# A two-layer S5/SSD trunk in fp32: x reloaded one tile a step, panel buffers shared between two phases, two more early pairs, a later spread

## The chip, the cores and the metric

The kernel runs on one core of one Trainium2 chip. The metric is the time of one execution on the device in microseconds (us). Names of engines: PE is TensorE, DVE is VectorE, ACT is ScalarE, POOL is GpSimd, SP is SyncE; in this kernel SP does nothing but issue DMAs.

## The reference

A trunk of two layers over one sequence of 1024 tokens and 1024 channels, all in float32. Each layer is a mixer (S5 in the first, Mamba-2 SSD in the second) followed by an MLP, each with an RMSNorm and a modulation (shift, scale, gate) in front, and a last RMSNorm closes it. What the change touches is the MLP:

```python
def _sq_relu_mlp(h, w1, w2):
    a = jax.nn.relu(h @ w1)      # w1: 1024 x 4096
    return (a * a) @ w2          # w2: 4096 x 1024
...
h = _modulate(_rmsnorm(x, norm_mlp_g[i]), sh2, sc2)
x = x + g2 * _sq_relu_mlp(h, mlp_w1[i], mlp_w2[i])
```

## The kernel before

**Arithmetic.** Every fp32 product is made of three matmuls of fp32r parts: `split` has ACT cast a tile to its high part (L84) and DVE subtract to get the low part (L85), and `mm3` multiplies high by high, high by low and low by high (L117 to L119). Both MLP products are done in 2x2 blocks with seven block products in place of eight, so there are panels that are sums and differences of blocks.

**The two MLP phases.** The up phase (`Up`) goes through 16 pairs m of column blocks of w1. `rows` loads and combines the weights of a pair, `pair` does its products and writes seven panels of the result (`put`, `minus`) to HBM scratch `bscr`, on POOL's DMA queue. A pair m below `UPS` has two of its seven products done earlier: while `up_second` (a generator) still builds the panels t1, t2, t3, t4 and b22 of h, each of its yields runs one `early(m)`, 24 matmuls whose results go to `sscr` and `cscr`; `pair` loads them again (L552, L553, the tiles `s` and `b12`) and does 60 matmuls. A pair m from `UPS` on does all of its 84. With `UPS` 12, the pairs 12 to 15 are of the second sort.

The down phase (`mlp_down`) has seven products q of eight steps s. One step is 24 matmuls that read one weight unit of w2 and one panel: `raw_w` and `raw_b` load them on SP's queue, three steps ahead; `prepare` splits them, two steps ahead (`h01h` and `h11h` are the high parts of a panel of step 0, `h21h` and `h31h` of step 1, `h41h` and `h51h` of step 2, `h61h` and `h71h` of step 3; step 4 reuses the tiles of step 0, and so on). After a product `evacuate` adds its four banks to x. x is not kept over the up phase: `up_save` writes it to `hscr` (named `xscr` in `mlp_down`), and in steps 2 to 5 of the first product `x_load` (L267) brings it back, 16 tiles of 256 KB, four a step, on SP's queue.

**Buffers.** Pool `K.wz` lives over both phases of an MLP, pool `K.br` only over the down phase (it is made after the pools `K.to` and `K.tp` of the up phase are released). A panel is a tile `br` of `K.br`, four buffers. The tiles `a22h` and `a22l` of the up phase lie in `K.wz`, two buffers each.

**Order.** The code is written as one stream, and a scheduler orders each engine's instructions from it, so that an SP row can stand ahead of one that the code has earlier. An engine, and SP's queue too, then works strictly in its order: a row that waits holds all rows behind it. SP's DMAs share eight completion semaphores in turn, so that a DMA also waits until the one eight before it has landed.

**The norm behind the first MLP.** `mid` is `norm_steps` (L200), a generator that is advanced two yields a step in product 5: squares of x summed to `ss`, column sums on PE, `rsqrt` on DVE in some ten small operations (`rsy`, L137 to L143), two yields, then `spread` (L156), four small matmuls (eight in the trace) that PE can do only when `rsy` is there, then the scaled tiles. `up_second` has two yields of the same kind ahead of its first use of `pb`.

Of the kernel before, what the change touches and what calls it, by code (L numbers as in the profile page):

```python
# [11 lines left out]
F32 = mybir.dt.float32  # L12
F32R = mybir.dt.float32r
# [6 lines left out]
P = 128  # L20
D = 1024
L = 1024
HT = 512
KT = D // P
EARLY = 5
DOWN = "b11", "t3", "t2", "b22", "t1", "t4", "b21"
UPS = 12
EPS = 1e-5
MAGIC = 12582912.0
TWO_PI = 6.283185  # L30
# [22 lines left out]
def half_of(half):  # L53
    return slice(half * HT, half * HT + HT)


def blk(i, n=P):
    return slice(i * n, i * n + n)
# [19 lines left out]
def tmp(K, name):  # L78
    return K.tmp.tile([P, 512], F32, tag="t", bufs=6, name=name)
# [51 lines left out]
def rsqrt(K, y, v):  # L131

    V = K.nc.vector
    n = v.shape[1]
    i = K.tmp.tile([P, n], I32, tag="rsi", name="rsi")
    t = K.tmp.tile([P, n], F32, tag="rst", name="rst")
    V.tensor_scalar(i, v.bitcast(I32), 1, None, op0=ALU.logical_shift_right)  # L137
    V.tensor_scalar(i, i, -1, 0x5F3759DF, op0=ALU.mult, op1=ALU.add)
    yy = i.bitcast(F32)
    for _ in range(3):  # L140
        V.scalar_tensor_tensor(t, yy, -0.5, yy, op0=ALU.mult, op1=ALU.mult)
        V.tensor_tensor(t, t, v, op=ALU.mult)
        V.scalar_tensor_tensor(y, t, 1.5, yy, op0=ALU.add, op1=ALU.mult)  # L143
        yy = y
# [55 lines left out]
def norm_steps(K, x, half, each, bank, order):  # L200

    nc = K.nc
    ss = K.br.tile([P, HT], F32, tag="ss", name="ss", bufs=1)
    for n, k in enumerate(order):
        if n == 0:
            nc.scalar.activation(ss, x[k][half], AF.Square)
        else:
            sq = tmp(K, "sq")
            nc.scalar.activation(sq, x[k][half], AF.Square)
            nc.vector.tensor_tensor(ss, ss, sq, op=ALU.add)  # L210
        yield
    yield
    pt = bank(K)
    for j in range(4):
        nc.tensor.matmul(pt[:, j:j + 1], ss[:, blk(j)], K.ones, start=True, stop=True)
    v = K.tmp.tile([P, 4], F32, tag="rsv", name="rsv")
    nc.vector.tensor_scalar(v, pt[:, 0:4], 1.0 / D, EPS, op0=ALU.mult, op1=ALU.add)
    y = K.tmp.tile([P, 4], F32, tag="rsy", name="rsy")
    rsqrt(K, y, v)
    yield  # L220
    yield
    pb = spread(K, y, bank)
    for k in range(KT):
        each(k, pb)
        yield
# [15 lines left out]
def h_tile(K, k, half, s, dtype=F32R):  # L241

    nm = f"h{k}{half}{'hl'[s]}"
    return K.hp.tile([P, HT], dtype, tag=nm, name=nm)
# [19 lines left out]
def x_load(K, x, src, ks=range(KT)):  # L264
    for k in ks:
        for f in range(2):
            K.nc.sync.dma_start(x[k][f], src[k, :, half_of(f)])  # L267
# [141 lines left out]
def up_second(K, pan, pool, x, G, sh, save):  # L409


    nc, V = K.nc, K.nc.vector

    def panel(nm):
        return [
            tuple(pool.tile([P, HT], F32R, tag=f"{nm}{j}{s}", name=f"{nm}{j}{s}") for s in "hl") for j in range(4)
        ]

    pan.b22 = [(h_tile(K, 4 + j, 1, 0), h_tile(K, 4 + j, 1, 1)) for j in range(4)]
    pan.t1 = [(h_tile(K, j, 1, 0), h_tile(K, j, 1, 1)) for j in range(4)]  # L420
    pan.t4, pan.t3, pan.t2 = panel("t4"), panel("t3"), panel("t2")
    up_save(K, x, 1, save)
    dsh = K.tmp.tile([P, 4], F32, tag="dsh", name="dsh")
    V.tensor_tensor(dsh, sh[:, 4:8], sh[:, 0:4], op=ALU.subtract)
    pb = rstd_half(K, [x[k][1] for k in range(KT)])
    yield
    yield
    for j in range(4):
        t11, t12, t21, t22 = x[j][0], x[j][1], x[4 + j][0], x[4 + j][1]
        for k in (j, 4 + j):  # L430
            V.scalar_tensor_tensor(x[k][1], x[k][1], G[:, k:k + 1], pb, op0=ALU.mult, op1=ALU.mult)
        V.tensor_tensor(t11, t12, t11, op=ALU.subtract)
        t2 = tmp(K, "t2")
        V.scalar_tensor_tensor(t2, t22, sh[:, 4 + j:5 + j], t11, op0=ALU.add, op1=ALU.subtract)
        split(K, *pan.t2[j], t2)
        V.scalar_tensor_tensor(t21, t21, sh[:, 4 + j:5 + j], t2, op0=ALU.add, op1=ALU.subtract)
        yield
    for j in range(4):
        t12, t22 = x[j][1], x[4 + j][1]
        V.scalar_tensor_tensor(t12, t22, dsh[:, j:j + 1], t12, op0=ALU.add, op1=ALU.subtract)  # L440
        split(K, *pan.t3[j], t12)
        if j % 2:
            yield
    for j in range(4):
        split(K, *pan.t1[j], x[j][0])
    yield
    for j in range(4):
        split(K, *pan.t4[j], x[4 + j][0])
    yield
    for j in range(4):  # L450
        shift_split(K, x[4 + j][1], pan.b22[j], sh[:, 4 + j:5 + j])
    yield
    yield
# [8 lines left out]
class Up:  # L462
# [9 lines left out]
    def bank(self, m):  # L472
        K = self.K
        return (K.ps if m % 4 < 2 else K.psb).tile([P, 512], F32, tag="ps", name="px")
# [39 lines left out]
    def early(self, m, pan):  # L514

        nc = self.K.nc
        u0 = unit(self.K, self.w1[of_pair(m)[0]])
        X, Z = self.bank(m), self.second_bank()
        self.product(X, u0, 0, pan.b11, True)
        s1 = self.held(X, "s1")  # L520
        nc.gpsimd.dma_start(self.sscr[m], s1)
# [3 lines left out]
    def rows(self, m, pool, late):  # L525

        K, V, g = self.K, self.K.nc.vector, SimpleNamespace()
        r0, r1 = [unit_raw(K, self.w1[i]) for i in of_pair(m)]
        g.u0 = unit_of(K, r0) if late else None
        g.a22 = tuple(pool.tile([P, HT], F32R, tag="a22" + s, name="a22" + s, bufs=2) for s in "hl")  # L530
        split(K, *g.a22, r1[:, HT:])
        V.tensor_tensor(r1[:, HT:], r1[:, 0:HT], r1[:, HT:], op=ALU.add)
        V.tensor_tensor(r1[:, 0:HT], r0[:, 0:HT], r1[:, 0:HT], op=ALU.subtract)
        V.tensor_tensor(r0[:, 0:HT], r1[:, HT:], r0[:, 0:HT], op=ALU.subtract)
        V.tensor_tensor(r0[:, HT:], r0[:, HT:], r0[:, 0:HT], op=ALU.subtract)
        g.u1 = unit_of(K, r0)
        g.u2 = unit_of(K, r1)
        return g

    def pair(self, m, g, pan, ahead):  # L540

        K = self.K
        X = self.bank(m)
        if g.u0:
            s = None
            self.product(X, g.u0, 0, pan.b11, True)
            b12 = self.held(X, "s1")
            Z = self.second_bank()
# [33 lines left out]
def mlp_down(K, pool, x, bscr, w2, gate, xscr, mid, extra):  # L582
# [7 lines left out]
    nc, V = K.nc, K.nc.vector  # L590
# [18 lines left out]
        return raws  # L609

    def raw_b(q, s):
        t = pool.tile([P, 2, HT], F32, tag="br", name="br", bufs=4)
        nc.sync.dma_start(t, bscr[q][s].rearrange("a p t -> p a t"))
        return t

# [66 lines left out]
    prepare(1)  # L682
    norms = iter(())
    X = None
    for n, (q, s) in enumerate(steps):
        load(n + 3)
        if q == 0 and 1 < s < 6:
            for k in (s - 2, s + 2):
                x_load(K, x, xscr, [k])
        prepare(n + 2)  # L690
        (wh, wl), b = ready.pop(n)
        if s == 0:
            X = X if q == 4 or q == 2 else banks(q)
            if q == 0:
                first = X
            if q in (2, 4):
                X = first
        for j in range(2):
            for i in range(4):
                c = blk(2 * i + j)  # L700
                mm3(
                    K, X[i], [(wh[:, c], wl[:, c], *b[j])],
                    q not in (2, 4) and s == 0 and j == 0, s == 7 and j == 1, more=True,
                )
        if s == 7:
            for i in range(4):
                evacuate(q, i, X[i])
        if q == 4 and s == 7:
            norms = mid(0, lambda K: K.ps.tile([P, 512], F32, tag="ps", name="pn"), range(KT))
        elif q == 5 or q == 6 and s < 3:  # L710
            next(norms, None)
            next(norms, None)
        elif q == 6:
            if s == 3:
                drain(norms)
                norms = mid(1, pss, [1, 3, 5, 7, 0, 2, 4, 6])
            if s < 7:
                next(norms)
        extra()
# [680 lines left out]
def trunk(ctx: ExitStack, tc: tile.TileContext, io, out):  # L1400
# [26 lines left out]
    K.bscr = [[[scr(f"b{i}{q}{s}", [2, P, HT]) for s in range(8)] for q in range(7)] for i in range(2)]  # L1427
    K.cscr = scr("cscr", [UPS, P, HT])
    K.sscr = scr("sscr", [UPS, P, HT])
    K.hscr = [scr(f"hscr{i}", [8, P, L]) for i in range(2)]  # L1430
# [10 lines left out]
    def mlp(i, x, xa, up, pan, gate, mid, cond=None, mods=(), gates=()):  # L1441
# [8 lines left out]
        for m in range(16):  # L1450
            ahead = []
            up.pair(m, rows, pan, lambda: m < 15 and ahead.append(up.rows(m + 1, K.wz, m + 1 >= UPS)))
            rows = ahead and ahead[0]
# [118 lines left out]
    def entry(i, x, G, sh):  # L1572
# [3 lines left out]
        def mid(f):  # L1576
            if f == 0:
                up.pan = up_first(K, x, G, sh, K.hscr[i])
            else:
# [4 lines left out]
                for _ in up_second(K, up.pan, K.tp, x, G, sh, K.hscr[i]):  # L1584
                    up.early(m, up.pan)
                    m += 1
                assert m == UPS

# [187 lines left out]
```

## Time and profile before

| what | value |
|---|---|
| time, median of 3 runs | 2564.22 us (2563.97 to 2564.57) |
| time of the profiled execution | 2565.46 us |
| its span in the trace | 2563.6 us |
| PE busy | 2453.4 us, 96% of the span, 11624 matmuls |
| DVE busy | 1914.1 us, 75% |
| ACT busy | 1151.5 us, 45% |
| POOL busy | 192.2 us, 7% |
| DMA queue of SP | 390.54 MB, 47.4% of the 16 DMA engines' time |
| DMA queue of POOL | 96.49 MB, 11.2% |

The span is what the trace covers; the profiled execution's own time is 1.9 us longer. PE is busy nearly all of the time, so the time can change where PE stands idle, and where its granted clock is below full. The idle time of the other engines counts only where PE waits for them.

### The profile page before, as it was taken

Reading aid. Unit: us, or ns where it says so; the run is one execution under the profiler, and the core shown is the slowest. Engines: PE = TensorE matmul, PEld = TensorE weight load, DVE = VectorE, ACT = ScalarE, POOL = GpSimd, SP = SyncE. Lnnn points to the kernel's source line nnn. Section 1 sums busy time; section 2 is a strip of 40 time slices with the busy share of each in tenths; the row PEclk is TensorE's granted clock in tenths of the full one; section 3 lists DMA queues with packets and bytes.
Section 4 is the critical chain, followed back from the end, with each engine's and each line's share of the span. In section 5 each row is a group of like instructions: output and inputs, shape, how many; then the busy total and the mean of one; then the engine's idle time right before and its main releaser. Section 6 shows DMA issues by size and latency. Waiting matters only on the chain.

```text
span 2563.6 us, 32608 instructions
## 1 busy us (share of the span) xinstructions
PE 2453.4 (96%) x11624; PEld 1964.4 (77%) x11624; DVE 1914.1 (75%) x3269; ACT 1151.5 (45%) x1903; POOL 192.2 (7%) x360
## 2 busy tenths in 40 slices
PE   7999999999997999999999999999999999799997
PEld 2787788777785888777888888878887778588886
DVE  8797754968777997958596868788687777576664
ACT  4586412743433443534464655544264443244442
POOL 0010000122220000100000000000011222100000
PEclk8999999999998999999999999999999999899998
DMA  6576772457759979723555554574236665873762
GB/s 240 157 165 175 243 234 86 156 206 259 255 183 338 314 260 317 251 75 114 160 158 158 160 175 141 181 245 131 86 128 210 224 217 183 303 218 126 259 204 68
DMA packets 284322, 497.49 MB, mean 194 GB/s; under 512 B 21760, under 2 KB 162048, under 8 KB 284160
## 3 DMA queue, kind: packets, MB, share of 16 engines
q1 hardware_dynamic: 245376, 390.54, 47.4%
q0 software_dynamic: 29184, 96.49, 11.2%
q10 hardware_dynamic: 9600, 8.39, 1.0%
q8 instruction: 91, 1.49, 0.2%
q14 instruction: 71, 0.58, 0.1%
HBM read 360.07 MB, written 131.07 MB: 192 GB/s over the span
## 4 chain that ended last, share of the span: by engine, by line
issue 41%; PE 36%; DVE 9%; DMA 9%; POOL 2%; ACT 2%; SPq 0%; POOLq 0%; DVEq 0%; ACTq 0%
PE pd L118 3%; PE pd L117 3%; PE pd L119 3%; PE py L117 3%; DMA ada<-in_ada 3%; PE py L118 3%; PE py L119 3%; DMA raw<-in_w 2%; PE px L117 2%; PE px L119 2%; PE px L118 2%; DVE wlo L85 2%; PE pm L117 1%; PE pm L119 1%; PE pv L119 1%
## 5 line engine op out<-in xcount | busy, mean ns | idle before, releaser
L84 ACT CAST whi<-raw 128x1024 fp32r<-128x1024 f32 x241 | 250.8, 1047 | 345.8 <-PE pd L118 145.0
L85 DVE TENSOR_TENSOR wlo<-raw,whi 128x1024 fp32r<-128x1024 f32 x241 | 292.8, 1216 | 113.7 <-ACT whi L84 112.9
L333 DVE SCALAR_TENSOR_TENSOR ada<-ada,cond 128x1024 f32<-128x1024 f32 x88 | 107.1, 1220 | 52.1 <-DMA ada<-in_ada 51.9
L498 ACT ACTIVATE s<-s 128x512 f32<-128x512 f32 x72 | 45.5, 632 | 171.4 <-DVE s L496 171.3
L1229 DVE SCALAR_TENSOR_TENSOR cacc<-cr,conv,cacc 128x1024 f32<-128x1024 f32 x72 | 91.6, 1278 | 0.9 <-ACT cacc L1210 0.8
L390 POOL DMA_DIRECT2D hscr<-x x32 | 17.4, 542 | 958.2 <-DVE x L730 754.9
L1282 ACT ACTIVATE L<-csb,cs 128x128 f32<-128x128 f32 x224 | 69.9, 390 | 39.8 <-DMA csb<-csr 39.7
L505 POOL DMA_DIRECT2D b<-s x96 | 52.0, 542 | 346.0 <-ACT s L499 244.2
L496 DVE TENSOR_TENSOR s<-s,px 128x512 f32<-128x512 f32 x56 | 38.3, 683 | 52.3 <-PE px L119 29.9
L496 DVE TENSOR_TENSOR s<-s,pv 128x512 f32<-128x512 f32 x40 | 27.4, 686 | 49.6 <-PE pv L119 49.4
L117 PE MATMUL py<-h01h,whi 128*128 128x512 f32 x64 | 27.3, 427 | 31.5 <-ACT h01h L84 31.5
L505 POOL DMA_DIRECT2D b<-tt x96 | 52.0, 542 | 46.1 <-DVE tt L510 33.4
L499 ACT ACTIVATE s<-s 128x512 f32<-128x512 f32 x72 | 45.6, 633 | 2.3
L1233 ACT ACTIVATE cth<-cacc 128x512 f32<-128x512 f32 x48 | 27.7, 624 | 40.3 <-DVE cacc L1229 40.3
L84 ACT CAST h01h<-br 128x512 fp32r<-128x512 f32 x28 | 17.4, 620 | 57.2 <-DMA br<-b 28.8
L1209 ACT COPY cr<-pd 128x512 f32<-128x512 f32 x48 | 27.8, 580 | 31.8 <-PE pd L119 31.6
L665 DVE SCALAR_TENSOR_TENSOR x<-py,mod,x 128x512 f32<-128x512 f32 x40 | 27.2, 744 | 20.0 <-PE py L119 20.0
L117 PE MATMUL pd<-h00h,whi 128*128 128x512 f32 (+1 forms) x97 | 39.9, 414 | 2.1 <-ACT h00h L237 1.8
L1302 DVE SCALAR_TENSOR_TENSOR y<-xs,cst,pm 128x128 f32<-128x128 f32 x128 | 38.2, 340 | 4.8 <-PE pm L1299 4.8
L1100 ACT ACTIVATE gt<-pd,bgh 128x512 f32<-128x512 f32 x16 | 11.0, 685 | 65.0 <-PE pd L119 65.0
L117 PEld LDWEIGHTS py<-h01h,whi 128*128 128x128 f32 x64 | 13.1, 204 | 35.2 <-ACT h01h L84 32.4
L117 PE MATMUL pd<-h01h,whi 128*128 128x512 f32 x97 | 39.4, 406 | 0.5 <-DVE h61h L730 0.5
(991 smaller groups left out, 8185.6 us busy)
## 6 DMA issues: line engine op xcount, KB each, us to landing
raw<-in_w SPq DMA_DIRECT2D x200, 512.0 KB, 4.6
br<-b SPq DMA_DIRECT2D x112, 512.0 KB, 4.9
ada<-in_ada SPq DMA_DIRECT2D x96, 512.0 KB, 5.0
b<-s POOLq DMA_DIRECT2D x96, 256.0 KB, 2.3
b<-tt POOLq DMA_DIRECT2D x96, 256.0 KB, 3.2
csb<-csr SPq DMA_DIRECT2D x32, 512.0 KB, 4.5
raw<-in_w_xbc SPq DMA_DIRECT2D x24, 512.0 KB, 4.7
xscr<-cacc SPq DMA_DIRECT2D x24, 512.0 KB, 2.7
```

Of the source, the lines that this page charges most:

```text
L84: K.nc.scalar.copy(hi, src)
L85: K.nc.vector.tensor_tensor(lo, src, hi.bitcast(F32), op=ALU.subtract)
L117: K.nc.tensor.matmul(ps, wh, xh, start=start and i == 0, stop=False, skip_group_check=more)
L118: K.nc.tensor.matmul(ps, wh, xl, start=False, stop=False, skip_group_check=more)
L119: K.nc.tensor.matmul(ps, wl, xh, start=False, stop=stop and i == n - 1, skip_group_check=more)
L333: K.nc.vector.scalar_tensor_tensor(r, r, 1.0, K.cond, op0=ALU.mult, op1=ALU.mult, accum_out=acc)
L496: nc.vector.tensor_tensor(t, t, p, op=ALU.add)
L498: nc.scalar.activation(t, t, AF.Relu)
L499: nc.scalar.activation(t, t, AF.Square)
L505: self.K.nc.gpsimd.dma_start(self.bscr[DOWN.index(nm)][m // 2][m % 2], t)
L1229: V.scalar_tensor_tensor(acc, cr[:, t:t + L], K.cw[:, i, t:t + 1], acc, op0=ALU.mult, op1=ALU.add)
L1282: nc.scalar.activation(Lm[:, r, :], cb[:, r, :], AF.Relu, bias=S.cs[:, c0 + r:c0 + r + 1], scale=-1.0)
```

## The change

Four edits, in both MLPs:

- x is reloaded in steps 1 to 16, one tile a step, on POOL's queue instead of SP's. Ahead of each load ACT copies one column of a panel part of that step into the tile, so that the load, which overwrites it, has to wait for the panel. The order of the tiles is x01, x21, x41, x61, then both halves of the odd ones, then x00, x20, x40, x60.
- The panels of the steps 0, 1, 4 and 5 of each product lie in `K.wz`, those of the steps 2, 3, 6 and 7 in `K.br`, two buffers each. The two a22 tiles become one tile of 128x1024 that shares the buffers of the former.
- `UPS` is 14, and `up_second` yields four times instead of twice ahead of its first use of `pb`.
- `norm_steps` yields four times instead of twice between `rsqrt` and `spread`.

```diff
-UPS = 12
+UPS = 14
...
     rsqrt(K, y, v)
-    yield
-    yield
+    for _ in range(4):
+        yield
     pb = spread(K, y, bank)
...
     pb = rstd_half(K, [x[k][1] for k in range(KT)])
-    yield
-    yield
+    for _ in range(4):
+        yield
...
-        g.a22 = tuple(pool.tile([P, HT], F32R, tag="a22" + s, name="a22" + s, bufs=2) for s in "hl")
+        a22 = pool.tile([P, 1024], F32R, tag="br", name="a22", bufs=2)
+        g.a22 = a22[:, 0:HT], a22[:, HT:]
...
     def raw_b(q, s):
-        t = pool.tile([P, 2, HT], F32, tag="br", name="br", bufs=4)
+        t = (K.wz, pool)[s // 2 % 2].tile([P, 1024], F32, tag="br", name="br", bufs=2)
+        t = t.rearrange("p (a t) -> p a t", a=2)
         nc.sync.dma_start(t, bscr[q][s].rearrange("a p t -> p a t"))
         return t
...
+    back = [(k, 1) for k in range(0, KT, 2)] + [(k, f) for k in range(1, KT, 2) for f in range(2)]
+    back += [(k, 0) for k in range(0, KT, 2)]
     for n, (q, s) in enumerate(steps):
         load(n + 3)
-        if q == 0 and 1 < s < 6:
-            for k in (s - 2, s + 2):
-                x_load(K, x, xscr, [k])
         prepare(n + 2)
         (wh, wl), b = ready.pop(n)
+        if 0 < n <= len(back):
+
+            k, f = back[n - 1]
+            nc.scalar.copy(x[k][f][:, 0:1], b[0][0][:, 0:1].bitcast(F32))
+            nc.gpsimd.dma_start(x[k][f], xscr[k, :, half_of(f)])
```

SP's rows of the kernel before, where the first MLP goes from its up phase to its down phase. `b000` is the panel of product 0, step 0, `b001` that of step 1, `b010` that of product 1, step 0; `hscr` holds x. The 16 loads of the first product's weights (`h00l` and so on) stand directly ahead of these rows.

```order
L607 DMA raw_7090<-in_w2 128x4x256
L267 DMA x00_6526<-hscr0_198 128x512
L267 DMA x01_6527<-hscr0_198 128x512
...
L267 DMA x31_6533<-hscr0_198 128x512
L613 DMA br_6563<-b000_84 128x2x512
L613 DMA br_6567<-b001_85 128x2x512
L613 DMA br_6571<-b002_86 128x2x512
L613 DMA br_6603<-b003_87 128x2x512
L332 DMA ada_6648<-in_ada 128x1024
L613 DMA br_6653<-b004_88 128x2x512
```

The fourteen x loads between the first two and the panels are cut to three rows here. The same place in SP's rows of the changed kernel; the first row stands ahead of the 16 weight loads.

```order
L615 DMA br_6573<-b000_84 128x2x512
...
L608 DMA raw_7053<-in_w2 128x4x256
L615 DMA br_6577<-b001_85 128x2x512
L615 DMA br_6663<-b004_88 128x2x512
...
L608 DMA raw_7200<-in_w2 128x4x256
L615 DMA br_6710<-b005_89 128x2x512
L615 DMA br_6851<-b010_92 128x2x512
L615 DMA br_6581<-b002_86 128x2x512
L615 DMA br_6613<-b003_87 128x2x512
L332 DMA ada_6658<-in_ada 128x1024
```

No x load stands in SP's rows any more, the panel of step 0 has moved ahead of the weight loads, and the panels of the steps 4 and 5 and of product 1's step 0, all in `K.wz`, now stand ahead of those of the steps 2 and 3.

PE's rows of the kernel before at the norm behind the first MLP, in product 5; `rsy` is what DVE's `rsqrt` leaves, `h31h` belongs to a panel of step 5 of that product and `h41h` to one of step 6.

```order
L117 MATMUL pn<-h31h,whi 128x512
L118 MATMUL pn<-h31l,whi 128x512
L119 MATMUL pn<-h31h,wlo 128x512
L156 MATMUL pn<-ident,rsy 128x128 x4
L117 MATMUL pm<-h41h,whi 128x512
```

The same place in the changed kernel.

```order
L117 MATMUL pn<-h51h,whi 128x512
L118 MATMUL pn<-h51l,whi 128x512
L119 MATMUL pn<-h51h,wlo 128x512
L156 MATMUL pn<-ident,rsy 128x128 x4
L117 MATMUL pm<-h61h,whi 128x512
```

The spread has moved one step, 24 matmuls, down PE's order; the order of DVE's small operations among the splits around it has not changed.

## Rows read from the trace of the kernel before

**Rows 1.** Page, busy time by engine

```profile
PE 2453.4 (96%) x11624; PEld 1964.4 (77%) x11624; DVE 1914.1 (75%) x3269; ACT 1151.5 (45%) x1903; POOL 192.2 (7%) x360
```

**Rows 2.** Waits of PE, whole span: us in total, times, longest

```profile
PE py L117 <- ACT h01h L84: 31.5, 2, 15.8
...
PE pn L156 <- DVE rsy L143: 8.1, 2, 5.6
PE px L117 <- DVE s L489: 7.7, 2, 4.0
PE px L117 <- ACT whi L84: 5.7, 7, 1.4
```

**Rows 3.** Timeline of PE, up to down phase, both MLPs: start, duration, instruction [idle before]

```profile
781.53 0.40 PE L119 MATMUL px<-h71h,wlo 128*128 128x512 f32 x1
797.77 0.79 PE L117 MATMUL py<-h01h,whi 128*128 128x512 f32 x1 [15.85 <-ACT h01h L84]
...
803.76 0.39 PE L118 MATMUL py<-h11l,whi 128*128 128x512 f32 x1
...
806.30 0.39 PE L117 MATMUL py<-h21h,whi 128*128 128x512 f32 x1
...
2232.01 0.79 PE L117 MATMUL py<-h01h,whi 128*128 128x512 f32 x1 [15.65 <-ACT h01h L84]
```

**Rows 4.** Chain that ended last, same stretch, first MLP: start, us, what

```profile
774.09 6.29 DMA raw<-in_w
...
780.39 8.28 DMA x<-hscr
...
788.69 8.39 DMA br<-b
```

**Rows 5.** Timeline of SP's queue, same stretch: start, us from first to last issue

```profile
777.07 10.85 SPq L267 DMA_DIRECT2D x<-hscr  x14
```

**Rows 6.** Windows, PE, PEld, DVE, ACT, POOL busy, then PEclk, DMA share, GB/s

```profile
780.00:800.00 20.00, 4.15 (x14) 2.72 (x13) 9.49 (x16) 4.08 (x8) 3.24 (x6) 0.67 1.05 399
820.00:1040.00 220.00, 220.00 (x962) 180.54 (x961) 190.24 (x295) 91.74 (x144) 4.33 (x8) 1.00 0.88 300
1060.00:1080.00 20.00, 19.60 (x77) 16.16 (x78) 16.11 (x25) 10.68 (x16) 2.17 (x4) 0.84 0.46 155
```

**Rows 7.** Tile br, whole span, time to landing

```profile
DMA to landing us min/median/max: 3.4/4.9/8.9
```

**Rows 8.** Groups by line and form, 820 to 1040 us of the down phase

```profile
L85 DVE TENSOR_TENSOR h01l<-br,h01h 128x512 fp32r<-128x512 f32 x10 | 6.8, 684 | 0.0
L84 ACT CAST h01h<-br 128x512 fp32r<-128x512 f32 x10 | 6.2, 620 | 11.4 <-issue 7.1 <-ACT h71h L84 1.7 <-PE pn L119 1.4
```

**Rows 9.** DMA issues, 800 to 1100 us: count, KB, median us to landing

```profile
br<-b SPq DMA_DIRECT2D x51, 512.0 KB, 5.3
...
rscr<-x POOLq DMA_DIRECT2D x12, 256.0 KB, 6.3
```

**Rows 10.** Timeline of PE, pair 0 of the up phase, first MLP

```profile
530.27 0.50 PE L117 MATMUL px<-h01h,whi 128*128 128x512 f32 x1 [3.64 <-DVE s L489]
...
534.25 0.40 PE L118 MATMUL px<-h31l,whi 128*128 128x512 f32 x1
```

**Rows 11.** Chain that ended last, pair 0, first MLP

```profile
521.43 1.15 DVE wlo L85
...
523.14 6.27 DMA s<-sscr
```

**Rows 12.** Groups by line and form, early pairs, 360 to 520 us

```profile
L85 DVE TENSOR_TENSOR wlo<-raw,whi 128x1024 fp32r<-128x1024 f32 x18 | 21.9, 1220 | 12.8 <-ACT whi L84 12.8
...
L489 DVE TENSOR_TENSOR s1z<-s,pv 128x512 f32<-128x512 f32 x11 | 7.5, 682 | 0.6 <-PE pv L119 0.6
```

**Rows 13.** Timeline of PE at the norm behind the first MLP

```profile
1060.40 2.07 PE L156 MATMUL pn<-ident,rsy 128*128 128x128 f32 x8 [5.61 <-DVE rsy L143]
```

## The prediction

> **What bounds the kernel now.** I read the busy times first: PE is busy 96% of the span [rows 1]. The change neither adds nor removes a matmul, so all it can move is PE's idle time and the stretches where PE's granted clock is low. The second view is therefore the waits of PE, longest in total first [rows 2]. Of its rows, three lie where an edit lies: 31.5 us in two waits for `h01h`, the first panel of the down phase; 7.7 us in two waits of the up phase's first pair for `s`; and 5.6 us, the longest of the waits for `rsy`. The fourth, 5.7 us in seven short waits for `whi`, is what pairs cost whose early products are already done.
>
> The third view is PE's timeline at the first of these places [rows 3]. The last up matmul begins at 781.53 and the first down matmul at 797.77, after 15.85 us of idleness. That is not all: from 797.77 to 803.76 PE does 13 matmuls, 0.46 us each, and from 803.76 to 806.30 11 matmuls, 0.231 us each. So after the stall PE runs at the lower of its two clocks (1.2 GHz) and loses 6.0 - 13 x 0.231 = 3.0 us more. The second MLP has the same stall, 15.65 us; its slow stretch I take as 2.7.
>
> Why the panel is late stands in the chain [rows 4]: three transfers, each waiting for the one ahead of it. A weight load issued at 774.09 takes 6.29 us; an x load that had to wait for it, 8.28; and the panel of step 0, which had to wait for that, 8.39. SP's queue issues 14 x loads over 10.85 us first [rows 5], and the panels stand behind all of them. In that stretch the 16 DMA engines are full, 1.05 busy at 399 GB/s [rows 6].
>
> **The transition, edits on x and on the panels.** In the changed order no x load is ahead of a panel, and the panel of step 0 goes to `K.wz` before the up phase ends, so it waits for none of the weights. Step 1's panel waits for the splits of step 0's, into tiles which the last pair frees some 24 matmuls, 5.5 us, before its end: about 777, and it lands 4.9 us later (median, [rows 7]), by 782. So the steps 0 and 1 can run right behind the up phase, from 781.9 to 781.9 + 2 x 24 x 0.231 = 793.0.
>
> Then comes something new. The panel of step 2 waits for nothing itself, but it stands on SP's queue behind that of product 1's step 0, which waits until DVE has split step 4's panel; those splits write tiles that step 0 reads, so they wait for PE's end of step 0, 781.9 + 5.5 = 787.4. Two casts and one subtraction, 0.62 + 0.62 + 0.68 [rows 8], bring it to 789.3, two issues to about 790. Landing in the down phase is 5.3 us [rows 9], the cast 0.62: PE gets step 2 at 796. I add 0.5, because one bank of step 0 is freed by ACT's last work of the up phase, which in the changed order stands behind the casts of step 1's panel (between nothing and 1.2 us). So step 2 begins at about 796.5 instead of 806.30 + 24 x 0.231 = 811.8: 15.3 us gained, and a new stall of 3 us, whose slow clock I put at 0.8, between nothing and the 3.0 above. Net 14.5; for the second MLP, with the same order and a stall smaller by 0.5, 14. Sum **28.5**. Bounds for one MLP: with the shortest landing (3.4), no late bank and no slow clock 17.5; with the longest (8.9), 1.2 for the bank and 3.0 of slow clock 8.
>
> The tied x loads cost nothing by themselves: one tile a step is 256 KB in 5.5 us, 48 GB/s, beside 300 GB/s with the engines 0.88 busy and PE never idle [rows 6]. The 16 copies of one column are bounded by the casts of 512 columns, 16 x 0.62 = 10 us, on an ACT that is busy 92 of 220 us there; were that cover gone, they would delay casts by 10 us an MLP at the most. They are queued ahead of later casts, which wait for PE anyway. POOL's queue has behind an x load only later x loads and the last panels of the up phase, of which the first is read in step 7, 38 us on.
>
> On splitting the x traffic off to another queue, the Trainium skill (DMA: Bandwidth & Descriptors, Issuing engines are not separate DMA queues) says that DMAs of all engines share the same 16 DMA engines, and that another issuing engine saves only issue time. The trace agrees as to the engines: they are full while x comes. By that rule alone the edit would buy little; what it buys here comes by the order, the ties keep 14 of 16 tiles out of the transition.
>
> **The first pair, edit on the early pairs.** PE waits 3.64 us for `s`, and 8 of the matmuls behind are slow: from 530.27 to 534.25 there are 11, which take 1.4 us more than 11 x 0.231 [rows 10]. The load of `s` is issued at 523.14 and takes 6.27; ahead of it is a weight load that waited for DVE's `wlo` [rows 11]. So DVE is behind PE, and catches up in early pairs: one is 5.5 us of PE but 1.22 + 0.68 us of DVE [rows 12]. Two more of them give DVE 2 x 3.6 = 7.2 us, of which 3.64 would do. The loads are gated by buffers as well as by DVE, and `s` is still behind weight loads, so I leave 1.5 us of stall, without slow clock: 3.64 + 1.4 - 1.5 = 3.5, and 4 for the second MLP (its stall is 7.7 - 3.6 = 4.0). Sum **7.5**; bounds 0 (PE and DVE shift together) and 10.5 (no stall left).
>
> **The spread, edit on the norm.** PE waits 5.61 us for `rsy` [rows 13]; then the eight spread matmuls and those behind them run slowly. PEclk is 0.84 over 1060 to 1080 [rows 6], that is 20 x 0.16 = 3.2 us lost at most; I take 2.2. A step later is 5.5 us later, and DVE's order is unchanged, so nearly nothing of the wait is left; for what is, 0.8. Gain 5.6 + 2.2 - 0.8 = **7**; bounds 0, if DVE is held by something else, and 8.8. Late next would be the scaled tiles behind the spread; the generator's remaining yields still fit ahead of product 6's drain.
>
> **What it costs.** Four pairs in all change from 84 to 60 matmuls. The seven waits for `whi` over some 24 such pairs are 0.24 us a pair, so 4 x 0.24 = **1 us** worse; bounds 0.5 and 5.6 (the longest wait, 1.4, each time). Their early products have moved, not grown. The reloads, 1.5 MB a pair, lie beside PE's work.
>
> **The sum.** -28.5 - 7.5 - 7 + 1 = -42. The profiled execution took 2565.46 us, 1.2 above the median of the runs, so 2523.5 by it, 2522 by the median. I say **2522 us**.
>
> **Rivals.**
> 1. *The new stall is deep.* Step 2's panel is stuck behind the wait on PE, and the pair-0 wait stays. Then each transition gains 8 instead of 14.5, the first pairs nothing: 2564 - 16 - 7 + 1 = 2542. For it: the queue order; against it: 8.9 us is the longest landing, and it came while the x loads filled the engines. If only one of the two holds, 2530 to 2535.
> 2. *The transfers are the limit, not the order*: x, panels and weights need the same bytes, and what is taken from the transition collides later. The 14 x loads are 3.7 MB, 9.2 us at 399 GB/s; if those come back as waits, each MLP gains only 15.9 + 3 - 3.8 - 9.2 = 6, and 2564 - 12 - 7.5 - 7 + 1 = 2538.5. The rule of the Trainium skill quoted above would have it so. Against it: 0.88 busy and no wait of PE from 820 to 1040.
> 3. *Slower*: the x tiles, now one a step on POOL's queue, come after `evacuate` wants them. The first four have three to seven steps, the next eight as many or more. The longest median landing on that queue is 6.3 us [rows 9], little over one step. It becomes slower when a load takes over 24 us, so that evacuations of products 0, 1 and 3 hold the banks in both MLPs: six stalls must each cost 7.5 us to eat 42. With 9 us each, 2576. Nothing in the trace speaks for such landings.
> 4. *The early pairs and the spread do nothing*, the transition as forecast: 2564 - 28.5 + 1 = 2536.5.
>
> **How the numbers follow.** Forecast 0.55, with a range of its own from 2513 to 2529; rival 1 and its halves 0.15, rival 2 0.1, rival 4 0.13, rival 3 0.05, no change 0.02. The three sums of gains at their upper bounds (35 + 10.5 + 8.8) give 2510; the rivals reach 2542. I take **2510 to 2542**. A change under 0.2%, 5 us, can hardly be told from none here; by the cases faster 0.92, same 0.03, slower 0.05.
>
> **What would show it.** In the changed profile: at the first down matmul no wait above 1 us; a wait of 2 to 4 us for `h41h` 11 us later, in both MLPs; in SP's timeline the panels without x loads ahead of them; the wait for `s` under 2 us; the wait for `rsy` under 1. Wrong would be a wait above 5 us for `h41h`, a low clock behind it, waits for x in the evacuations, or waits of casts behind the copies.

## The result and the profile after

The changed kernel takes 2532.22 us (median of 4 runs, 2527.48 to 2533.94), against 2564.39 of the kernel before (median of 4): ratio 0.9872, 95% interval 0.9857 to 0.9888. The forecast was 2522 within 2510 to 2542; 32 of its 42 us came. The time lies outside the narrower range, 2513 to 2529, that the prediction gave its main case. PE's waits in the profile after, the longest in total:

```profile
PE py L117 <- ACT h41h L84: 10.7, 2, 5.9
...
PE px L117 <- ACT s L487: 6.1, 2, 3.1
PE pn L156 <- DVE rsy L143: 5.5, 2, 3.0
PE px L117 <- ACT whi L84: 5.3, 6, 1.4
...
PE px L117 <- DVE s L489: 3.0, 2, 1.9
```

Against [rows 2]: the 31.5 us for `h01h` are gone and 10.7 us for `h41h`, the panel of step 2, are new; the waits for `s` of the first pair and for `rsy` have shrunk; the waits for the copies `s` of the last pair (L487) have grown to 3.02 and 3.05. Of the two waits for `rsy` the one of 3.0 us lies at the norm behind the first MLP; the other, 2.5 us, lies at the last norm, is there in the kernel before too, and is left out below. PE's timeline at the transitions:

```profile
780.92 0.40 PE L119 MATMUL px<-h71h,wlo 128*128 128x512 f32 x1
781.15 0.40 PE L117 MATMUL py<-h01h,whi 128*128 128x512 f32 x1
...
791.97 0.39 PE L119 MATMUL py<-h31h,wlo 128*128 128x512 f32 x1
797.17 0.79 PE L117 MATMUL py<-h41h,whi 128*128 128x512 f32 x1 [4.81 <-ACT h41h L84]
...
2211.89 0.79 PE L117 MATMUL py<-h41h,whi 128*128 128x512 f32 x1 [5.93 <-ACT h41h L84]
```

The first down matmul follows the last up matmul after 0.23 us where [rows 3] has 15.85 us of idleness, and the steps 0 and 1 run through. Then comes the new stall, as foreseen, but of 4.81 and 5.93 us instead of 3 and 2.5. Its chain in the first MLP:

```profile
787.36 0.56 DVE wlo L85
...
787.97 0.70 DVE h11l L85
...
788.68 0.37 SPq L615
...
789.10 7.38 DMA br<-b
...
796.50 0.63 ACT h41h L84
```

The chain goes back to `h11l`, the split of step 4's panel, on which SP's row for product 1's panel waits; step 2's panel is issued right behind it at 789.10. That is 7.95 us after the down phase begins, and the forecast had 8.1. What is longer is the landing: 7.38 us, not 5.3. In the second MLP it is 8.44:

```profile
2202.76 8.44 DMA br<-b
```

Where the time went, by the starts of PE rows that both traces have (each number is the length of a stage):

| stage | before | after | difference |
|---|---|---|---|
| start to the last up matmul, first MLP | 781.53 | 780.92 | -0.6 |
| to step 2 of the down phase | 30.22 | 16.25 | -14.0 |
| to the SSD mixer (`dtf`, L1150) | 357.43 | 354.71 | -2.7 |
| to the last up matmul, second MLP | 1046.79 | 1042.65 | -4.1 |
| to step 2 of the down phase | 29.71 | 17.36 | -12.4 |
| to the last norm (`ss`, L215) | 302.77 | 304.96 | +2.2 |
| to the end of the span | 15.15 | 15.35 | +0.2 |

The sum is -31.4, the difference of the spans (2563.6 and 2532.2). The third and the sixth stage hold the slow clock behind the new stalls: 14 matmuls take 6.1 us behind the first and 10 take 4.4 behind the second, 2.9 and 2.1 us more than at 0.23 us each.

### The profile page after: what moved, and what is told of

It reads as the page before. It is cut to its first block, busy times and chain, and to the rows that moved or that the text cites. A ratio compares the mean times of both kernels' runs of the same rounds, so it can differ in the third digit from the quotient of the medians.

```text
span 2532.2 us, 32780 instructions
## 1 busy us (share of the span) xinstructions
PE 2451.7 (97%) x11624; PEld 1965.7 (78%) x11624; DVE 1914.6 (76%) x3265; ACT 1167.9 (46%) x1955; POOL 213.7 (8%) x400
## 3 DMA queue, kind: packets, MB, share of 16 engines
q0 software_dynamic: 32384, 106.98, 12.4%
q10 hardware_dynamic: 9600, 8.39, 1.0%
## 4 chain that ended last, share of the span: by engine, by line
PE 74%; issue 8%; DVE 6%; DMA 6%; ACT 4%; POOL 2%; SPq 0%; DVEq 0%; POOLq 0%; ACTq 0%
PE pd L118 10%; PE pd L117 10%; PE pd L119 10%; PE py L117 4%; PE py L118 4%; PE py L119 4%; PE px L117 3%; PE pm L117 2%; PE pm L118 2%; PE pm L119 2%; PE px L119 2%; PE px L118 2%; PE pv L117 2%; PE pv L118 2%; PE pv L119 2%
## 5 line engine op out<-in xcount | busy, mean ns | idle before, releaser
L333 DVE SCALAR_TENSOR_TENSOR ada<-ada,cond 128x1024 f32<-128x1024 f32 x88 | 107.3, 1222 | 57.8 <-DMA ada<-in_ada 57.7
L498 ACT ACTIVATE s<-s 128x512 f32<-128x512 f32 x84 | 53.0, 631 | 158.5 <-DVE s L496 155.9
L499 ACT ACTIVATE s<-s 128x512 f32<-128x512 f32 x84 | 53.2, 633 | 2.7
L119 PE MATMUL pd<-h10h,wlo 128*128 128x512 f32 (+1 forms) x97 | 39.3, 405 | 0.0
L622 DVE TENSOR_TENSOR raw<-raw 128x1024 f32<-128x1024 f32 x16 | 19.6, 1225 | 26.0 <-DMA raw<-in_w 26.0
L118 PE MATMUL pd<-h00l,whi 128*128 128x512 f32 (+1 forms) x97 | 38.8, 400 | 0.4 <-DVE h00l L238 0.4
```

What stands on the lines that cost most here:

```text
L118: K.nc.tensor.matmul(ps, wh, xl, start=False, stop=False, skip_group_check=more)
L119: K.nc.tensor.matmul(ps, wl, xh, start=False, stop=stop and i == n - 1, skip_group_check=more)
L333: K.nc.vector.scalar_tensor_tensor(r, r, 1.0, K.cond, op0=ALU.mult, op1=ALU.mult, accum_out=acc)
L498: nc.scalar.activation(t, t, AF.Relu)
L499: nc.scalar.activation(t, t, AF.Square)
```

## The experiments

The ratios are to the kernel before, run on the same chip. First the edits one at a time, each put alone into the kernel before.

**The reload of x alone** (`back`, the tying copy and POOL's load in; `x_load` in steps 2 to 5 out).

> The kernel before with the reload of x alone changed (one tile a step, tied, on POOL's queue); panels in four buffers of K.br as before, 12 early pairs, two yields. Theory of the queue's order: the panels stand right behind the weights on SP's queue, step 0's is issued near 779 instead of 788.7 and lands in 5 to 8 us, so the wait of 15.85 us falls to 4 to 6, and so in the second MLP: 2564 - 22 = 2542 us, most of what the whole change brings. Theory of the transfers: x's 3.7 MB were 9 us of full engines; spread out, the same gain. If x's place on SP's queue doesn't matter, 2560 or more.

Measured 2560.53 us, ratio 0.9975 (0.9965 to 0.9986): 6 us, not 22. PE and SP's queue:

```profile
784.77 0.40 PE L119 MATMUL px<-h71h,wlo 128*128 128x512 f32 x1
796.54 0.79 PE L117 MATMUL py<-h01h,whi 128*128 128x512 f32 x1 [11.37 <-ACT h01h L84]
```
```profile
775.83 14.49 SPq L607 DMA_DIRECT2D raw<-in_w  x5
790.41 2.07 SPq L613 DMA_DIRECT2D br<-b  x4
```

Without x, five weight loads, which wait for buffers, hold SP's queue for 14.49 us, and the panels go out at 790.41, against 788.69 in [rows 4]. This profile's up phase ends later, too: counted from the start of the last up matmul (784.77 here, 781.53 before), the panel of step 0 goes out after 5.6 us instead of 7.2, and it lands in 5.43 us instead of 8.39. Both theories overrated the edit: x alone was not what held the panels back.

**The panel buffers alone** (with the a22 tile that shares them; the diff shows the panels' part).

```diff
-        t = pool.tile([P, 2, HT], F32, tag="br", name="br", bufs=4)
+        t = (K.wz, pool)[s // 2 % 2].tile([P, 1024], F32, tag="br", name="br", bufs=2)
```

> The kernel before with the panel buffers alone changed (half of them in K.wz, shared with a22), x reloaded as before by SP in steps 2 to 5. Steps 0 and 1 run right behind the up phase; the panel of step 2 stands behind ten x loads. Theory of the queue's order: it is issued near 790 to 793, so PE waits 6 to 10 us for h41h instead of 15.85 for h01h, a gain of 7 to 10 us an MLP with the clock: 2546 to 2550 us. Theory of the transfers: x's bytes collide with the panels, the wait is nearer to 10 or more: 2550 to 2556 us.

Measured 2538.87 us, ratio 0.9893 (0.9873 to 0.9914), a gain of 27 us, more than expected and most of the whole change.

```profile
804.27 0.79 PE L117 MATMUL py<-h41h,whi 128*128 128x512 f32 x1 [5.22 <-ACT h41h L84]
```
```profile
793.98 9.60 DMA br<-b
```

With ten x loads still ahead of step 2's panel, the stall is 5.22 us (5.72 in the second MLP), about that of the changed kernel. The panel is issued 6.0 us into the down phase, which begins at 788.01, and lands in 9.60; in the changed kernel it was issued after 7.95 and landed in 7.38. And PE waits only 0.28 us for `rsy`, with two yields.

**The early pairs alone** (`UPS = 14`, four yields in `up_second`).

> The kernel before with 14 early pairs and four yields in up_second alone. By the forecast's step: the waits for s (3.64 and 4.03 us) fall to 1.5 each and their slow clock goes, two more pairs an MLP wait a little for whi: 2564 - 6.5 = 2558 us. By the trace of the changed kernel: the up phase there is 0.7 us longer in the first MLP and 3.3 shorter in the second, so 2561 to 2562 us; the wait for the copies s of the last pair (2.18 and 2.42 us) grows by 0.5 to 1.

Measured 2555.43 us, ratio 0.9953 (0.9937 to 0.9969): 12 us.

```profile
534.51 0.50 PE L117 MATMUL px<-h01h,whi 128*128 128x512 f32 x1 [0.89 <-DVE s L489]
...
1962.75 0.50 PE L117 MATMUL px<-h01h,whi 128*128 128x512 f32 x1 [0.51 <-DVE s L489]
```

The waits for `s` are nearly gone. In the changed kernel 1.95 and 1.02 us of them are left. The single profile of the changed kernel had made the edit look too small.

**The norm's yields alone, and the whole change without them.**

> The kernel before with four yields in norm_steps alone. The spread stands one step, 5.5 us, later on PE; the wait for rsy, 5.61 us, falls to 0 to 0.5 and the low clock behind it goes: a gain of 6 to 7 us, ratio 0.9975. Rival: DVE is late by what it waits for ada's transfers, in an order that shifts with the edit, and the wait stays at 3 or more: a gain of 0 to 3, ratio 0.999 to 1.

Measured 2562.23 us, ratio 0.9986 (0.9975 to 0.9998): 3.6 us.

```profile
801.43 0.79 PE L117 MATMUL py<-h01h,whi 128*128 128x512 f32 x1 [15.78 <-ACT h01h L84]
...
1064.56 0.38 PE L156 MATMUL pn<-ident,rsy 128*128 128x128 f32 x1 [0.69 <-DVE rsy L143]
```

The wait went as expected, and PEclk is 1.00 in the 20 us behind it (0.84 in [rows 6]). In this profile the stage from step 2 to the SSD mixer is 7.5 us shorter than before (349.91 against 357.43); the runs, which decide, gave 0.5 to 6.4 us.

> The changed kernel with two yields in norm_steps as before; the other three edits stay. If PE now comes to the spread earlier and the transfers that DVE waits for do not, the wait for rsy is the 3.0 us of the changed kernel plus the step, 8 to 9 us, and the ratio to the kernel before is 0.990 to 0.991 instead of 0.9872. If the step of 24 matmuls is hidden anyway, the wait is 3 to 6 and the ratio stays below 0.989. In the kernel with the panel buffers alone (e3_pools) there was no such wait with two yields; if that comes from the panel buffers and not from x's early reload, there is none here either.

Measured 2538.56 us, ratio 0.9900 (0.9879 to 0.9921). First this kernel, then the changed one:

```profile
782.24 0.40 PE L117 MATMUL py<-h01h,whi 128*128 128x512 f32 x1
...
1050.25 0.58 PE L156 MATMUL pn<-ident,rsy 128*128 128x128 f32 x1 [5.86 <-DVE rsy L143]
```
```profile
1051.53 1.35 PE L156 MATMUL pn<-ident,rsy 128*128 128x128 f32 x8 [3.00 <-DVE rsy L143]
```

In the kernel before, the edit takes the wait from 5.61 to 0.69 us; in the changed kernel from 5.86 to 3.00. The wait with two yields is that of the kernel before, not the 8 to 9 us of the first theory: PE comes to the spread earlier, but so does `rsy`, by 10 us each (1050.25 against 1060.40). What differs is what the edit does to `rsy` itself. Counted from the first down matmul, `rsy` is there after 268.0 us with two yields and 270.4 with four; without the other edits, after 262.6 and 263.1. So, in these single profiles, part of the step is given back. In time the edit is worth some 7 us here by the two ratios (0.9900 and 0.9872), but their intervals overlap.

**x as before, the other edits in** (e12_xsp, the complement of the first experiment).

> The changed kernel with x reloaded as before (SP's queue, steps 2 to 5, four tiles a step); panel buffers, early pairs and both sets of yields as changed. If the tied reload is worth what the forecast gave it, x stands ahead of the panels of steps 2 and 3 again, the waits for h41h are 8 us or more and the ratio to the kernel before is 0.990 or more. If the gains of the single parts add up (0.9893 for the buffers, 0.9953 for the early pairs, 0.9986 for the yields), the ratio is 0.983, below the whole change's 0.9872, and the tied reload costs some 10 us net; the waits for h41h are then 5 to 6 us as in e3_pools and there is no wait for rsy.

Measured 2523.75 us (5 runs), ratio 0.9840 (0.9826 to 0.9853): faster than the whole change, whose interval begins at 0.9857. So the tied reload costs about 8 us in this company.

```profile
794.38 0.79 PE L117 MATMUL py<-h41h,whi 128*128 128x512 f32 x1 [5.72 <-ACT h41h L84]
```

The stall at step 2 is about that of the changed kernel, and there is no wait for `rsy`. From step 2 to the SSD mixer this kernel takes 349.15 us, the changed one 354.71. Between step 2 and the spread PE waits in neither. Most of these 5.6 us come at the spread: in the changed kernel a wait of 3.0 us and a lower clock behind it (PEclk 0.91 over the next 20 us, 1.00 here). Whether the copies on ACT or the x transfers bring that about was not tried.

**The changed kernel without the ties** (the copy left out, the loads of x on POOL's queue as soon as their tiles are free).

> The changed kernel without the 16 copies that tie the x loads to panels: they stay on POOL's queue in the same order, but go as soon as their tiles are free, so most of x's 4 MB come while the panels of steps 2 and 3 load. SP's order is the same. Theory of the transfers: step 2's panel takes 5 to 9 us longer than its 7.4 and 8.4 us, waits of 9 to 13 us for h41h instead of 4.81 and 5.93: ratio to the kernel before 0.991 to 0.994. If only SP's queue mattered, no change from the changed kernel's 0.9872.

Measured 2546.08 us, ratio 0.9932 (0.9908 to 0.9956).

```profile
803.39 0.80 PE L117 MATMUL py<-h41h,whi 128*128 128x512 f32 x1 [15.02 <-ACT h41h L84]
...
2231.27 0.79 PE L117 MATMUL py<-h41h,whi 128*128 128x512 f32 x1 [17.00 <-ACT h41h L84]
```
```profile
785.12 17.59 DMA br<-b
...
2213.18 17.39 DMA br<-b
```

SP's order is that of the changed kernel; only when x's bytes come is different, and the stall is 10 to 11 us longer. In the first MLP step 2's panel is issued 7.95 us into the down phase, as in the changed kernel, and takes 17.59 us to land instead of 7.38. If x goes over another queue, the tie is needed: what collides is the transfers.

**The order of SP's queue, in two steps** (e1_order, e5_order2). First the panels of steps 2 and 3 ahead of two others (`third.ins` is the DMA of step 3's panel), then ahead of step 4's panel and three weight loads as well.

```diff
+        if (q, s) in ((0, 5), (1, 0)):
+            with K.tc.issue_after(third.ins):
+                nc.sync.dma_start(t, bscr[q][s].rearrange("a p t -> p a t"))
+            return t
```

> The changed kernel with one ordering edge in each MLP: SP issues the panels of steps 5 and of product 1's step 0 only behind the panel of step 3, so that the panels of steps 2 and 3 stand right behind the weight loads and no longer behind a row that waits for PE. Theory of the queue's order: step 2's panel is issued about 7 us earlier (782 instead of 789.1 in the first MLP), lands before step 1 ends even if it takes 8 us, and the waits for h41h (4.81 and 5.93 us in the changed kernel) and the slow clock behind them (about 2.5 us each) go: 2532 - 16 = 2516 us. Theory of the transfers: the 16 DMA engines are full there (1.03 busy, 391 GB/s), the panel only takes longer, half or more of the waits stays: 2524 to 2532 us.

Measured 2525.93 us, ratio 0.9836 (0.9817 to 0.9856).

```profile
791.00 0.50 PE L117 MATMUL py<-h41h,whi 128*128 128x512 f32 x1 [1.52 <-ACT h41h L84]
...
2198.19 0.59 PE L117 MATMUL py<-h41h,whi 128*128 128x512 f32 x1 [3.18 <-ACT h41h L84]
```
```profile
779.65 1.62 SPq L621 DMA_DIRECT2D br<-b  x2
```
```profile
2185.17 12.32 DMA br<-b
```

The panel is issued at 779.65, 1.4 us into the down phase instead of 7.95, and the stall falls from 4.81 to 1.52 and from 5.93 to 3.18. In the second MLP it takes 12.32 us to land (2185.17 to 2197.49). Both theories hold a part: the place in the queue sets when the panel starts, and what is in flight with it how long it takes.

> The kernel of e1_order with more edges: SP issues step 4's panel and the weight loads of product 1's steps 5 to 7 behind step 3's panel too, so that 2 MB less stand ahead of the panels of steps 2 and 3. In e1_order step 2's panel was issued at 779.65 and took 10.7 us (12.3 in the second MLP) with the engines 1.05 busy. Theory of the transfers: 2 MB at 364 GB/s are 5.5 us, the panel lands before step 1 ends, the waits for h41h (1.52 and 3.18 us) and their slow clock go: another 5 to 8 us, ratio to the kernel before near 0.981. Theory of the order alone: nothing more to gain, 0.9836 as e1_order, or worse by the delayed weights.

Measured 2513.58 us, ratio 0.9797 (0.9773 to 0.9822), another 10 us, though the intervals just overlap. The stall is 1.52 us in both MLPs, and ACT's timeline shows what it is now:

```profile
791.75 0.62 ACT L84 CAST whi<-h40l 128x512 fp32r<-128x512 f32 x1 [4.32 <-PE py L118]
792.28 0.61 ACT L84 CAST whi<-h50l 128x512 fp32r<-128x512 f32 x1
792.80 0.61 ACT L84 CAST h41h<-br 128x512 fp32r<-128x512 f32 x1
```

The panel is there; its cast stands behind two casts of step 6's weights, the first of which waits for PE's step 1. The wait for `rsy` is gone too.

> The kernel of e5_order2 with two yields in norm_steps as before. There was no wait for rsy in e5_order2 (four yields) and none in e3_pools (two yields), in both of which the DMA engines moved 324 to 328 GB/s in the stretch ahead of the spread, against 298 to 312 in the kernels with a wait. If the wait comes from DVE lagging behind the transfers it needs, and SP's order decides that, there is little or none here either (0 to 2 us) and the ratio stays near 0.980. If the two more yields are what hid it in e5_order2, the wait is 3 to 6 us and the ratio 0.9815 to 0.983.

Measured 2518.61 us (e9_order2n2), ratio 0.9813 (0.9788 to 0.9837), and no wait for `rsy` with two yields: in this order PE does not need the norm edit there. The time is not told apart from the 0.9797 with four yields.

**The order of ACT's queue, in two steps** (e10_order3, e11_order4), on top of e5_order2 (`K.copied`: the last pair's copy; `fourth`: the cast of step 2's panel; `K.relu`: the read `r`; the second piece is in the second step only).

```diff
+            if q == 0 and s > 0:
+                with K.tc.issue_after(fourth.ins if s > 5 else K.copied):
+                    split(K, hi[:, c], lo[:, c], hd[j])
...
+            if s == 1 and not hasattr(fourth, "ins"):
+                with K.tc.issue_after(K.relu):
+                    split(K, *b[j], t[:, j])
```

> The kernel of e5_order2 with ordering edges on ACT: the casts of product 0's weights from step 1 on stand behind the last pair's copies s, and those of the steps 6 and 7 behind the cast of step 2's panel. In e5_order2 the copies stand behind casts that wait for weight loads, and PE waits 3.17 and 3.10 us for them and runs at the lower clock for some 1.5 to 2 us behind; h41h stands behind two casts that wait for PE's step 1, 1.52 us in each MLP. If a row that waits at the head of ACT's queue is the cause of both, the waits for s fall below 1 us, those for h41h to 0, and the time by 10 to 13 us: ratio 0.975. If the data itself is late, the waits stay and the ratio is 0.979 to 0.980.

Measured 2516.19 us, ratio 0.9804 (0.9789 to 0.9819): the waits for `s` and `h41h` went as expected, the time did not. A new wait had come:

```profile
778.58 0.62 ACT L84 CAST h21h<-br 128x512 fp32r<-128x512 f32 x1 [6.92 <-DMA br<-b]
...
779.62 0.59 ACT L574 ACTIVATE r<-px 128x512 f32<-128x512 f32 x1
```
```profile
780.26 0.50 PE L118 MATMUL py<-h01h,whi 128*128 128x512 f32 x1 [2.88 <-ACT r L574]
```

> The kernel of e10_order3 with one more edge on ACT: the casts of step 1's panel stand behind r, the last read of the up phase's last bank. In e10_order3 the waits for s and h41h were gone and a new one had come, 2.88 and 4.41 us for r, because r stood behind the casts h21h and h31h that wait for the panel's load, and step 0's last bank is the one that r reads. If that row at the head of ACT's queue is the cause, the wait falls below 1 us in both MLPs, no lower clock follows, and the time falls by 8 to 12 us: ratio 0.976 to 0.977. If the load of step 1's panel is what is late, PE waits for h21h instead, 1 to 3 us, and the ratio is 0.979 to 0.980.

Measured 2510.81 us, ratio 0.9788 (0.9772 to 0.9805), not told apart from 0.9797. The wait for `r` is gone, and the next stands in its place, 2.58 and 3.11 us, now for DVE's low part of step 2's panel:

```profile
789.70 0.50 PE L119 MATMUL py<-h41l,whi 128*128 128x512 f32 x1 [2.58 <-DVE h41l L85]
```

By its median this is the fastest kernel run: 55 us under the kernel before and about 21 under the change.

## Why the prediction was right, and what in it was wrong

**Right, with errors that offset each other.** Right were the sign, the range, and the main mechanism: the steps 0 and 1 now run behind the up phase, the panel of step 2 stands on SP's queue behind a row that waits for PE, and it is issued 8 us into the down phase. Changing SP's order alone took 3.29 and 2.75 us off the two stalls. But the range was wide, and the size came out by luck in part. Alone, the four parts bring 6, 27, 12 and 3.6 us by their ratios, about 49, where the forecast added up 42 and the whole brought 32. By the prediction's own signs it was partly wrong: one wait for `h41h` is above 5 us, the clock fell behind both, and the wait for `rsy` is not under 1. And 2532 lies among the 2530 to 2535 that the prediction gave to a half of its first rival.

**The transition, mis-sized.** "Landing in the down phase is 5.3 us [rows 9]" was a median of a stretch with the engines less full. Here it was 7.38 and 8.44, with them 1.03 and 1.01 busy:

```profile
785.00:805.00 20.00, 15.19 (x55) 11.79 (x54) 14.85 (x25) 6.49 (x14) 3.27 (x6) 0.83 1.03 391
```
```profile
2200.00:2220.00 20.00, 14.07 (x54) 10.91 (x53) 11.15 (x19) 6.99 (x15) 2.19 (x4) 0.83 1.01 355
```

So the stalls were 4.81 and 5.93 for 3 and 2.5, and the clock behind them fell (PEclk 0.83), for which the sum had 0.8 an MLP and 2.9 and 2.1 us were lost. The two terms, 28.5 in the forecast, measured 14.0 + 12.4 less 5.0 of slow clock, about 21. That is most of the 10 us that did not come. The bank that I gave 0.5 us cost nothing here; it showed, with 2.88 and 4.41 us, only in e10_order3, where ACT's read of it stood behind casts that waited for step 1's panel.

**The cause I named for the late panel was only half of it.** I read from [rows 4, 5] that x stood ahead of the panels and put x's removal and the buffers into one term. Alone, x's removal brings 6 us and the buffers 27. Without x, five weight loads waiting for buffers hold the queue about as long as x did. The tied reload, which I costed at nothing, costs some 8 us beside the other three edits; without it their parts nearly add up (43 us alone, 41 together). So the terms of the sum were not independent, as it took them to be.

**The first pair, too small.** 6.5 us net were forecast; alone the edit brings 12. The residual stalls are then 0.5 to 0.9 us, not 1.5, and the extra pairs cost nothing visible, where the sum had 1 us. In the changed kernel the residual stalls are 1.95 and 1.02, about the 1.5 each of the forecast. In the changed kernel's first MLP less is seen of it: the wait for the last pair's copies, which the forecast left unchanged, rose from 2.18 to 3.02 us and was followed by the low clock.

**The spread, its wait right alone and wrong in company.** "Nearly nothing of the wait is left" holds where the edit stands alone (0.69 us), though the runs there gave 3.6 us for the forecast 7. In the changed kernel 3.0 us of wait were left. The step that failed is that DVE would be as early as before because its order is unchanged: counted from the first down matmul, `rsy` is there after 262.6 us in the kernel before and after 270.4 in the changed one, 7.8 us later, while PE comes 10.4 us later (the step and the new stall). So only 2.6 of the 5.6 us of wait went. What fits all the kernels is that DVE waits for ada's transfers (`ada`, L333: tiles of `in_ada` that SP loads and DVE multiplies in between the splits). These windows are the stretch ahead of the spread, in the changed kernel, in e12_xsp and in e5_order2:

```profile
820.00:1033.00 213.00, 213.00 (x932) 174.86 (x932) 183.78 (x283) 88.95 (x145) 8.70 (x16) 1.00 0.90 308
```
```profile
815.00:1030.00 215.00, 215.00 (x941) 176.51 (x940) 197.78 (x304) 91.21 (x139) 4.32 (x8) 1.00 0.96 326
```
```profile
810.00:1020.00 210.00, 210.00 (x919) 172.37 (x918) 192.11 (x299) 92.06 (x149) 9.26 (x17) 1.00 0.96 334
```

Six kernels with no wait for `rsy`, or 0.28 us (panel buffers alone, e5_order2, e9_order2n2, e10_order3, e11_order4, e12_xsp), moved 326 to 336 GB/s there; all the others, among them the kernel with four yields alone and its 0.69 us, 291 to 316. From the start of the down phase to the spread DVE waited for ada 7.8 to 13.9 us in those six and 15.6 to 21.3 in the others. The changed kernel and e12_xsp:

```profile
DVE ada L333 <- DMA ada<-in_ada: 19.4, 17, 3.9
```
```profile
DVE ada L333 <- DMA ada<-in_ada: 7.8, 10, 2.0
```

That the queue's order lets fewer bytes through in the one case is what I take from this. It is not shown as the cause: which row holds it was not tried.

**Rivals.** The first, a deeper stall, and the second, transfers that collide later, each came in part: the stall was 5 us, and the untied kernel shows the collision in full. The third, x too late on POOL's queue, did not come: no wait for an x load stands in the changed profile. Nor did the fourth: the early pairs and the spread each bring time alone. The rule of the Trainium skill (DMA: Bandwidth & Descriptors, Issuing engines are not separate DMA queues), that another queue brings no engine of its own, is what the untied kernel shows in numbers: 15 and 17 us of stall, with SP's order unchanged and 17.6 and 17.4 us for one panel to land.

## What to carry to other kernels

When a stall goes, ask of each engine's queue what row stands at its head next and what that row waits for: here it was x, then weight loads, then a panel waiting for PE, then casts on ACT, then a bank, then DVE. Size a transfer by its landing in the stretch where it will run, with the engines as full as there, not by the median of a calmer one. Try the parts of a change alone and left out: one of four was a loss that the others hid.

## What was not expected of the hardware

After the same 1.36 us of idleness in an up pair, PE kept full speed in the profile before and fell to the lower clock in the changed kernel's. Before and after, first MLP:

```profile
649.56 0.50 PE L117 MATMUL px<-t20h,whi 128*128 128x512 f32 x1 [1.36 <-ACT whi L84]
...
650.85 0.40 PE L118 MATMUL pv<-t30l,whi 128*128 128x512 f32 x1
```
```profile
655.33 0.50 PE L117 MATMUL px<-t20h,whi 128*128 128x512 f32 x1 [1.36 <-ACT whi L84]
...
656.77 0.63 PE L118 MATMUL pv<-t30l,whi 128*128 128x512 f32 x1
```

In the second MLP it is the other way round: PEclk is 0.83 over 2080 to 2090 in the profile before, 1.00 over 2070 to 2080 in the one after. A fall from full speed over 10 us at 0.83 is 1.7 us, and whether it comes after a short stall differs from place to place. The up phase of the first MLP, from the first spread to the last up matmul, took 341.9 to 345.9 us in four kernels that are nearly alike there. A single profile can't settle a term of 2 to 4 us; the runs can.
